# Operand buffers of a projection and an attention as tiles of their own, with unused words between them

## The chip, the core and the metric

The kernel runs on one core of one Trainium2 chip. The time is the device time of one launch in microseconds. Two runs of the kernel before took 3833.39 and 3838.01 us, median 3835.7. Times below are counted from the start of the profiled execution's span.

## The reference

The reference is a two-layer trunk over 2304 tokens (256 of context, 2048 latent) of width 1024, in float32. Per layer:

```python
h = layer_norm(x) * (1.0 + scale) + shift
(hq, hff, hfb, hi, hgate, mcq, mckv, mkr, mgate,
 gq, gk, gv, gaf, gab, ggate) = split_cols(h @ w_in)
hg_lat, hg_ctx = bidirectional_recurrence(...)     # HGRN2, chunks of 64
gla_lat, gla_ctx = bidirectional_recurrence(...)   # gated linear attention
mla_lat = blockwise_attend(q, k, v)                # softmax attention, latent q and kv
x_new = layer_norm(DEEPNORM_ALPHA * x + gate * (y @ w_out)) * ln_g + ln_b
```

`y` is the three groups' outputs, normed or gated, side by side. The context tokens get the same treatment in the first layer only. All products are float32; the kernel makes each from three one-pass products of a high and a low part: `a b = ah bh + ah bl + al bh`.

## The kernel before, in words

Each layer runs three stages: `project` (normed activations times the input weights, the results staged in DRAM), `mix` (attention and the two recurrences side by side) and `output` (output projection, residual, post norm). In time: layer 0's projection from about 48 to 698.5 us, its mix to about 1640, its output to 1992; layer 1's projection from 1993 to 2611, its mix to about 3500, its output to the end.

**Projection.** Nine pairs of token tiles (256 tokens) in three blocks; for each block, twelve weight groups of 224 or 256 columns run against the block's pairs. `split_pair` (L396) turns a pair's activations `hf` into `hh` and `hl` ([128, 8, 256] each, four of either), `group_weights` (L342) loads a weight group and turns it into `wh` and `wl` (two of either). `group` (L404) has two forms of product: `natural` (L411, matmul L417) holds the tokens of h stationary and streams 256 weight columns; `transposed` (L421, matmul L428) holds 128 weight columns stationary and streams the 256 tokens. An L417 or L428 matmul is named `pj` after its result. ScalarE makes the high parts (a cast, through the helper `split`, L73 to L83, so many casts have line L77) and VectorE the low parts (L83), and ScalarE or VectorE stage the results (`stg`) for DRAM.

**Mix.** `mix` (L945) first reads the keys and values back from DRAM, in five pieces of 512 tokens (the last of 256) each: `cth`, `ctl`, `ks` for the scores, `cnh`, `cnl` for the weighted sum. Each piece passes through a raw buffer `kraw`; `kraw` and the query's `cq` share two buffers. `query_group` (L819) prepares two token tiles' queries: `cq` is split, multiplied into `pq` (24 matmuls, L838) and `pr` (12), 8 transposes give `ptq`, and the results are `qh`, `ql`, `rh`, `rl`. `attend` (L869) makes the scores `pss` from five products (L888 to L892: `cth qh`, `ctl qh`, `cth ql`, `ks rh`, `ks rl`), the exponentials `sx`, their transposes `ptp`, split into `ph` and `pl`, and the weighted sum `oc` (L913 to L917). The recurrences (`back_states`, `recur`) run between.

**Memory.** `Route` (L40) makes one pool per string that it is given, one behind the other in memory; a tag's buffers come from the pool that names the tag. A pool's space is given back at the end of a stage, and a tile placed there later waits for the users of exactly the tiles that it overlaps. In `project` of before, `hh hl` come first and `wh wl` last, above everything that mix or output uses. Byte offsets in a partition: hh at 33,376 + 8192 i, hl at 66,144 + 8192 i; wh at 196,384 and 204,576, wl at 212,768 and 220,960 in layer 0 (544 lower in layer 1); mix's cth, ctl, ks at 112,224 to 139,872; output's lnb, z, xto and wob between 91,008 and 136,064.

**Order of the work.** A scheduler places each instruction on its engine by priority and by when its inputs and buffers are expected to be ready; engines run in that order. `AHEAD` = 600 (L953) lets mix's key loads and first query come earlier than the place where they are written, `EARLY` = 1000 (L290) does so for the first weights and activations of layer 1's projection.

Of the kernel before, what the change touches and what calls it, by code (L numbers as in the profile page):

```python
# [7 lines left out]
F32 = mybir.dt.float32  # L8
F32R = mybir.dt.float32r
# [7 lines left out]
P = 128  # L17
# [14 lines left out]
def view(ap, offset, dims, parts=None):  # L32
    """A free-dimension pattern of its own on the tile behind ap."""
    pd = list(ap.ap[0])
    if parts is not None:
        pd[1] = parts
    return bass.AP(ap.tensor, ap.offset + offset, [pd] + [list(d) for d in dims])


class Route:  # L40
    """Tiles by tag, each from the pool that holds the tag: the order of pools is the order in memory."""
# [12 lines left out]
class Trunk:  # L54
# [17 lines left out]

    def split(self, hi, lo, src, hi_eng="act", lo_eng="dve"):  # L73
        """src = hi + lo with both parts in the tensor engine's one-pass format."""
# [10 lines left out]
    def rsqrt(self, pool, v, n, name):  # L85
        """(v + eps already added) ** -0.5 for a [P, n] tile."""
        r = pool.tile([P, n], F32, tag=name, name=name)
        self.nc.gpsimd.tensor_tensor(r, v, self.mhalf[:, :n], op=ALU.pow)
        return r

    def constants(self):
# [5 lines left out]
        # the gated heads' query scale, on the rows of the even and of the odd heads  # L97
# [11 lines left out]
    def scratch(self, l):  # L109
        """Layer l's arrays in DRAM, and its modulation columns."""  # L110
# [25 lines left out]
    def mod_first(self, S, R, ps, first):  # L136
        """Layer 0's shift and scale as columns."""
        nc, io = self.nc, self.io
        pm = [ps.tile([2, 512], F32, tag="pj", bufs=4, name="pm") for _ in range(4)]
        for k in range(KD):  # L140
            w = R.tile([P, 2 * D], F32, tag=("hh", "hl")[k % 2], bufs=4, name="wmod")
# [19 lines left out]
    def mod_rest(self, S0, S1, R, bm0):  # L161
        """Layer 0's gate and layer 1's modulation: products along the free dimension, one column block at a time."""
# [30 lines left out]
        bm = R.tile([P, 24], F32, name="bmd")  # L193
# [10 lines left out]
    def lower_bounds(self, S):  # L204
        """Layer 1's forget-gate floor: the running sum of the softmax over layers less its first term."""
# [20 lines left out]
    def gate_weights(self, l, S, R):  # L226
        """The low-rank gate weights stacked [hi; hi; lo], against gates stacked [hi; lo; hi]."""
# [9 lines left out]
    def latent_weights(self, l, S, R, ps):  # L237
        """The low-rank query and key weights joined: M_h = W_uq,h W_uk,h^T; and the rotary and value ones."""
# [28 lines left out]
    def project(self, l, S, after):  # L267
        """after: the next layer's arrays, where its modulation is worked out beside this projection."""
        nc, io = self.nc, self.io
        with ExitStack() as ctx:  # L270
            R = Route(lambda: self.pool(ctx), "hh hl", "stg gcat gq gkv",
                      "zaT ltn lkd zn zh ltt lqn jk ss rsk rsq ropt ropa ropb gxs gab",
                      "srow wmt jkm mp mc bmc bmd gcol pad", "wraw", "xt st mv ve rs hf", "wh wl")
            ps = Route(lambda: self.pool(ctx, psum=True), "tz", "pj", "tr", "px")
            npair = self.ntiles // 2
            blocks = [list(range(p0, min(p0 + 3, npair))) for p0 in range(0, npair, 3)]
            # the first two weight groups run side by side while the first block's tokens come in
# [9 lines left out]
            else:  # L287
                pad = R.tile([P, 64 * 64], F32, name="pad")
# [48 lines left out]
    # weight groups in the order in which they run: first column, number of columns  # L337
# [4 lines left out]
    def group_weights(self, l, R, g, first=False):  # L342
# [3 lines left out]
        wh = R.tile([P, KD, 256], F32R, tag="wh", bufs=2, name="wh")  # L346
        wl = R.tile([P, KD, 256], F32R, tag="wl", bufs=2, name="wl")
# [7 lines left out]
    def normed_pair(self, l, S, R, ps, pr, plain=False):  # L355
        """The modulated norm of two token tiles, transposed: [d, k, 256]; plain leaves out the modulation."""
# [39 lines left out]
    def split_pair(self, R, hf, hi_eng="dve"):  # L396
        hh = R.tile([P, KD, 256], F32R, tag="hh", bufs=4, name="hh")
        hl = R.tile([P, KD, 256], F32R, tag="hl", bufs=4, name="hl")
# [5 lines left out]
    def group(self, l, S, R, ps, g, w, h, pairs):  # L404
        """One weight group against a block's token pairs; yields after each pair."""
# [4 lines left out]
        def natural(pr):  # L410
            """[P, tile of the pair, 256]: tokens on partitions, n weight columns."""  # L411
# [9 lines left out]
        def transposed(pr):  # L421
            """[P, 128-column block, 256]: weight columns on partitions, the pair's tokens."""
# [12 lines left out]
        def by_tile(o):  # L435
            """[P, block, tile, 128] on a stage that holds tile by tile."""
# [58 lines left out]
    def rope(self, pool, out, src, t, per_tile):  # L495
        """Rotary positions by rows and columns. src [P, n, 64]; out [P, n, 2, 64] holds the result twice.
        n counts tiles from t on (per_tile), or heads of tile t."""
# [23 lines left out]
    def rms(self, pool, pj, n, tag):  # L521
        """[P, 2] reciprocal RMS over n columns of each tile of the pair."""
# [8 lines left out]
    def key_latents(self, S, pp, ps, pj, pr, xs):  # L531
        """RMS norm and rotary positions of a pair's key latents, and their transposes; the forget gates' inputs."""
# [52 lines left out]
    def gla_decay(self, S, pp, xs, pairs):  # L585
        """The forget gates exp(log_sigmoid(x) / 16), both directions of a block."""
# [14 lines left out]
    def head_rows(self, h):  # L601
        """(key slice in a [.., 3*128] natural tile, output rows, output column block, value block)"""
# [6 lines left out]
    def chunk_products(self, rp, rps, kT, vt, name):  # L609
        """Chunk by chunk [P, block, 64]: sum over the chunk's tokens of key x value for all heads."""  # L610
# [583 lines left out]
```

## Time and profile before

| | |
|---|---|
| runs, median | 3835.7 us |
| profiled execution, own span | 3840.8 us |
| TensorE (PE) busy | 3740.7 us, 97% |
| VectorE (DVE) busy | 2529.3 us, 66% |
| ScalarE (ACT) busy | 1452.2 us, 38% |
| GpSimd (POOL) busy | 187.3 us, 5% |
| mean granted TensorE clock | 0.989 |

A matmul's busy time in the profile (about 0.28 us for 256 columns) is longer than the distance between two starts, because matmuls overlap in the array; the distance between starts is read from the order in time. A clock of 1.00 is 2.4 GHz, 0.50 is 1.2 GHz.

### The profile page before, as it was taken

How to read it: one execution, taken by the hardware profiler on the slowest of the kernel's cores; microseconds unless marked ns; L12 is line 12 of the kernel's file. 1: busy time of each engine (PE TensorE's matmuls, PEld its weight loads, DVE VectorE, ACT ScalarE, POOL GpSimd, SP SyncE). 2: the span in 40 equal slices, each digit the busy share in tenths (PEclk: the TensorE clock that was granted, in tenths of full speed). 3: DMA queues.
4: the chain of work that ended last, by engine and by line, in shares of the span. 5: the costliest groups of instructions: out<-in, count | busy, mean ns of one | idle time of the engine just before them, and what ended most of it. 6: DMA issues, size and time to landing. Idle time of an engine off the chain costs nothing.

```text
span 3840.8 us, 82784 instructions
## 1 busy us (share of the span) xinstructions
PE 3740.7 (97%) x34152; PEld 3341.4 (87%) x34152; DVE 2529.3 (66%) x6956; ACT 1452.2 (38%) x2347; POOL 187.3 (5%) x194
## 2 busy tenths in 40 slices
PE   8899999999999999998999999999999999999899
PEld 5899999888888888887879999998888888888777
DVE  6763242577888888776765432426778888888566
ACT  3524242344444444442115252523444444444400
POOL 1000000000000000010110000000000000000111
PEclk9999999999999999999999999999999999999999
DMA  7775453323222212114435453523231212211232
GB/s 253 229 206 155 122 155 108 110 85 92 76 68 62 69 57 69 54 59 167 150 105 181 141 156 101 170 90 118 78 96 49 79 55 69 73 55 33 89 140 104
DMA packets 305850, 415.30 MB, mean 108 GB/s; under 512 B 43008, under 2 KB 235840, under 8 KB 304448
## 3 DMA queue, kind: packets, MB, share of 16 engines
q1 hardware_dynamic: 304032, 407.64, 33.8%
q8 instruction: 269, 4.41, 0.5%
q10 hardware_dynamic: 1440, 2.36, 0.2%
q14 instruction: 109, 0.89, 0.1%
HBM read 290.89 MB, written 119.03 MB: 107 GB/s over the span
## 4 chain that ended last, share of the span: by engine, by line
PE 71%; DVE 2%; DMA 2%; ACT 1%; issue 0%; POOL 0%; SPq 0%; DVEq 0%; ACTq 0%; POOLq 0%
PE pj L417 10%; PE pa L774 7%; PE ptp L924 6%; PE pj L428 5%; PE oc L917 4%; PE oc L913 4%; PE pzo L1069 3%; PE pzo L1070 3%; PE pzo L1071 3%; PE pss L888 3%; PE oc L914 3%; PE pss L889 3%; PE pss L891 3%; PE pss L890 3%; PE pss L892 3%; PE po L801 1%
## 5 line engine op out<-in xcount | busy, mean ns | idle before, releaser
L417 PE MATMUL pj<-wh,hl 128*128 128x256 f32 (+1 forms) x2224 | 623.0, 281 | 8.4 <-DVE hl L83 8.4
L417 PE MATMUL pj<-wh,hh 128*128 128x256 f32 (+1 forms) x2224 | 624.5, 281 | 2.0 <-DVE ve L369 1.2
L417 PE MATMUL pj<-wl,hh 128*128 128x256 f32 (+1 forms) x2224 | 623.1, 280 | 0.0
L77 ACT CAST ph<-ptp 128x512 fp32r<-128x512 f32 x580 | 333.2, 586 | 369.9 <-PE ptp L924 349.6
L83 DVE TENSOR_TENSOR pl<-ptp,ph 128x512 fp32r<-128x512 f32 x580 | 392.9, 686 | 111.2 <-ACT ph L77 109.9
L893 DVE TENSOR_SCALAR_CACHE_REDUCE sx<-pss 128x512 f32<-128x512 f32 (+1 forms) x648 | 399.2, 631 | 79.5 <-PE pss L892 74.2
L417 PEld LDWEIGHTS pj<-wh,hl 128*128 128x128 f32 x2224 | 421.5, 190 | 9.3 <-DVE hl L83 9.3
L417 PEld LDWEIGHTS pj<-wh,hh 128*128 128x128 f32 x2224 | 423.1, 190 | 2.7 <-DVE ve L369 1.6
L417 PEld LDWEIGHTS pj<-wl,hh 128*128 128x128 f32 x2224 | 422.3, 190 | 0.0
L924 PE MATMUL ptp<-ident,sx 128*128 128x128 f32 x2320 | 368.5, 275 | 17.2 <-ACT sx L903 17.2
L903 ACT ACTIVATE sx<-sx,nm 128x2304 f32<-128x2304 f32 (+1 forms) x136 | 288.4, 2121 | 173.5 <-DVE nm L899 171.4
L913 PE MATMUL oc<-ph,cnh 128*128 128x256 f32 x1160 | 346.0, 320 | 5.1 <-ACT ph L77 4.4
L83 DVE TENSOR_TENSOR wl<-wraw,wh 128x1024 fp32r<-128x1024 f32 (+1 forms) x144 | 169.6, 1211 | 238.8 <-ACT wh L77 238.7
L428 PE MATMUL pj<-hh,wh 128*128 128x256 f32 x1136 | 321.0, 283 | 0.0
L428 PE MATMUL pj<-hh,wl 128*128 128x256 f32 x1136 | 319.3, 281 | 0.0
L428 PE MATMUL pj<-hl,wh 128*128 128x256 f32 x1136 | 318.2, 280 | 0.0
L914 PE MATMUL oc<-ph,cnl 128*128 128x256 f32 x1160 | 301.9, 282 | 0.0
L924 PEld LDWEIGHTS ptp<-ident,sx 128*128 128x128 f32 x2320 | 272.8, 141 | 28.0 <-ACT sx L903 19.4
L774 PE MATMUL pa<-qa,km 64*64 64x64 f32 (+1 forms) x4896 | 279.3, 248 | 3.4 <-DVE qa L739 3.1
L888 PE MATMUL pss<-cth,qh 128*128 128x512 f32 (+1 forms) x648 | 269.4, 416 | 5.4 <-DVE sx L893 5.0
L917 PE MATMUL oc<-pl,cnh 128*128 128x256 f32 x1160 | 251.1, 297 | 7.0 <-DVE pl L83 6.8
L774 PEld LDWEIGHTS pa<-qa,km 64*64 64x64 f32 x4896 | 202.4, 134 | 58.4 <-issue 34.3
(241 smaller groups left out, 8035.7 us busy)
## 6 DMA issues: line engine op xcount, KB each, us to landing
wraw<-in_w_in_dram SPq DMA_DIRECT2D x132, 512.0 KB, 4.7
dnat<-stg SPq DMA_DIRECT2D x104, 256.0 KB, 2.1
vg<-dnat SPq DMA_DIRECT2D x34, 512.0 KB, 4.2
yt<-dy SPq DMA_DIRECT2D x34, 512.0 KB, 3.6
wmt<-in_w_modT_dram SPq DMA_DIRECT2D x64, 256.0 KB, 4.0
fa<-dF SPq DMA_DIRECT2D x36, 384.0 KB, 3.3
ka<-dK SPq DMA_DIRECT2D x36, 384.0 KB, 3.3
dK<-stg SPq DMA_DIRECT2D x36, 256.0 KB, 4.1
```

Of the source, the lines that this page charges most:

```text
L77: nc.scalar.copy(hi, src)
L83: nc.vector.tensor_tensor(lo, src, hi, op=ALU.subtract)
L417: nc.tensor.matmul(pj[:, j, :n], h[pr][a][:, k, tk], w[b][:, k, :n], start=(k == 0 and a + b == 0), stop=(k == KD - 1 and a == 1))
L428: nc.tensor.matmul(pj[:, j, :], w[b][:, k, cs], h[pr][a][:, k, :], start=(k == 0 and a + b == 0), stop=(k == KD - 1 and b == 1))
L774: nc.tensor.matmul(pa[rows, po:po + n], km[rows, sl, tk:tk + 64], mv, start=True, stop=True, tile_position=(64 * e, 64 * e))
L888: nc.tensor.matmul(pss[:, :n], G["qh"][hp][:, i, tk], K["cth"][:, ks], start=True, stop=False)
L893: nc.vector.tensor_scalar(sx[:, ks], pss[:, :n], SCALE, None, op0=ALU.mult, op1=ALU.max, accum_out=mx[:, nb:nb + 1])
L903: nc.scalar.activation(sx[:, :nk], sx[:, :nk], AF.Exp, bias=nm, accum_out=sm)
L913: nc.tensor.matmul(oc, K["cnh"][:, ks], ph[:, c, :], start=(kc + c == 0), stop=False)
L914: nc.tensor.matmul(oc, K["cnl"][:, ks], ph[:, c, :], start=False, stop=False)
L917: nc.tensor.matmul(oc, K["cnh"][:, ks], pl[:, c, :], start=False, stop=(kc + c == nch - 1))
L924: nc.tensor.transpose(pt[:, c, i, :], pexp[i][:, (kc + c) * P:(kc + c + 1) * P], self.ident)
```

## The change

In `project`, `wh` and `wl` move from the last pool to right behind `hh` and `hl`, and every one of the four `hh`, four `hl`, two `wh`, two `wl` becomes a tag with a pool of its own, in the order hh0 hl0, hh1 hl1, hh2 hl2, hh3 hl3, wh0 wl0, wh1 wl1. Four more tiles, of 8 to 64 words, stand between these pairs (all but hh3 and wh0); `fill` writes one column of each and nothing reads them. In `mix`, the same is done to qh and ql (four) and ph and pl (two), with gaps of 16 to 48 words; in layer 1 another one stands ahead of `rh rl`.

The new byte offsets in layer 0's projection: hh at 33,376, 49,824, 66,272 and 82,720, each hl 8192 behind; wh0 at 99,104, wl0 at 107,296, wh1 at 115,520, wl1 at 123,712 to 131,904. In layer 1: wh0 at 99,008, wl0 at 107,200, wh1 at 115,648, wl1 at 123,840 to 132,032. Mix's cth, ctl and ks lie at 112,416 to 140,064 (layer 0; 128 lower in layer 1).

The instructions are the same on all engines but GpSimd, which gets 17 memsets. Comments and docstrings are dropped, so line numbers shift (L77 becomes L83 in the changed kernel, L83 becomes L89, L966 becomes L984).

```diff
+    def fill(self, pool, *names):
+        for name in names:
+            n = int(name.split("_")[1])
+            self.nc.gpsimd.memset(pool.tile([P, n], F32, name=name)[:, 0:1], 0.0)
...
-            w = R.tile([P, 2 * D], F32, tag=("hh", "hl")[k % 2], bufs=4, name="wmod")
+            w = R.tile([P, 2 * D], F32, tag=f"h{'hl'[k % 2]}{k // 2 % 4}", name="wmod")
...
-        bm = R.tile([P, 24], F32, name="bmd")
+        bm = R.tile([P, 24], F32, tag="bmc", name="bmd")
...
-            R = Route(lambda: self.pool(ctx), "hh hl", "stg gcat gq gkv",
+            self.nh, self.nw = 0, 0
+            gaps = ("ha_16", "hb_16", "hc_16", "wa_8") if l == 0 else ("ha_8", "hb_8", "hc_8", "wa_64")
+            R = Route(lambda: self.pool(ctx), "hh0", "hl0", gaps[0], "hh1", "hl1", gaps[1], "hh2", "hl2", gaps[2],
+                      "hh3", "hl3", "wh0", "wl0", gaps[3], "wh1", "wl1", "stg gcat gq gkv",
                       "zaT ltn lkd zn zh ltt lqn jk ss rsk rsq ropt ropa ropb gxs gab",
-                      "srow wmt jkm mp mc bmc bmd gcol pad", "wraw", "xt st mv ve rs hf", "wh wl")
+                      "srow wmt jkm mp mc bmc bmd gcol pad", "wraw", "xt st mv ve rs hf")
+            self.fill(R, *gaps)
...
-                pad = R.tile([P, 64 * 64], F32, name="pad")
+                pad = R.tile([P, 62 * 64], F32, name="pad")
...
-        wh = R.tile([P, KD, 256], F32R, tag="wh", bufs=2, name="wh")
-        wl = R.tile([P, KD, 256], F32R, tag="wl", bufs=2, name="wl")
+        wh = R.tile([P, KD, 256], F32R, tag=f"wh{self.nw % 2}", name="wh")
+        wl = R.tile([P, KD, 256], F32R, tag=f"wl{self.nw % 2}", name="wl")
+        self.nw += 1
...
-        hh = R.tile([P, KD, 256], F32R, tag="hh", bufs=4, name="hh")
-        hl = R.tile([P, KD, 256], F32R, tag="hl", bufs=4, name="hl")
+        hh = R.tile([P, KD, 256], F32R, tag=f"hh{self.nh % 4}", name="hh")
+        hl = R.tile([P, KD, 256], F32R, tag=f"hl{self.nh % 4}", name="hl")
+        self.nh += 1
...
-            ap = Route(lambda: self.pool(ctx), "os mx nm sm ri", "mg", "ym", "ph pl", "cth ctl ks", "cq cqh cql",
-                       "qn ropt ropa ropb", "rh rl", "qh ql", "cnh cnl", "sx")
+            self.nq, self.np = 0, 0
+            gaps = ("pa_48", "qa_16", "qb_16", "qc_16", "") if l == 0 else ("pa_16", "qa_16", "qb_16", "qc_16", "ra_32")
+            ap = Route(lambda: self.pool(ctx), "os mx nm sm ri", "mg", "ym", "ph0", "pl0", gaps[0], "ph1", "pl1", "cth ctl ks", "cq cqh cql",
+                       "qn ropt ropa ropb", gaps[4], "rh rl", "qh0", "ql0", gaps[1], "qh1", "ql1", gaps[2], "qh2",
+                       "ql2", gaps[3], "qh3", "ql3", "cnh cnl", "sx")
+            self.fill(ap, *[g for g in gaps if g])
```

The tags qh, ql, ph and pl change in `query_group` and `attend` as hh and hl do in `split_pair`.

The scheduler's order moves with the buffers. First place: ScalarE at the end of layer 0's projection. Of the kernel before, where the first casts of the keys stand among the projection's stages (`stg`) and weight casts:

```order
L453 ACT_TABLE_LOAD
L453 ACTIVATE stg<-pj 128x2x2x128
L77 CAST cth<-kraw 128x512 x2
L77 CAST wh<-wraw 128x1024 x2
L453 ACTIVATE stg<-pj 128x2x2x128
L77 CAST cth<-kraw 128x512 x2
L459 ACT_TABLE_LOAD
L459 ACTIVATE stg<-pj 128x2x2x128
L460 ACTIVATE stg<-pj 128x2x2x128
L77 CAST cth<-kraw 128x256
L77 CAST cqh<-cq 128x512
```

Of the changed kernel, the same casts (line L83 there; `DMA kraw` are loads that ScalarE's queue issues):

```order
L497 ACTIVATE stg<-pj 128x512 x3
L83 CAST wh<-wraw 128x1024 x2
L497 ACTIVATE stg<-pj 128x512 x6
L83 CAST cth<-kraw 128x512 x4
L83 CAST cth<-kraw 128x256
L984 DMA kraw<-dkT_92 128x512
L83 CAST cqh<-cq 128x512
L984 DMA kraw<-dkT_92 128x512
L986 CAST ks<-kraw 128x512
L984 DMA kraw<-dkT_92 128x512
L986 CAST ks<-kraw 128x512
L83 CAST qh<-pq 128x512
```

The casts of cth, which stood ahead of the projection's last weight groups, now stand behind its last six stages; behind these rows come the other ks, qh, three cnh, then the first rh. TensorE in the changed kernel, at the same place, behind the last pj and the first query products:

```order
L903 MATMUL pss<-cth,ql 128x512 x2
L863 MATMUL pr<-urh_1183,cqh 128x256
L863 MATMUL pr<-url_1184,cqh 128x256
L863 MATMUL pr<-urh_1183,cql 128x256
L863 MATMUL pr<-urh_1183,cqh 128x256
L863 MATMUL pr<-url_1184,cqh 128x256
L863 MATMUL pr<-urh_1183,cql 128x256
L874 MATMUL ptq<-ident,qn 128x128 x4
L904 MATMUL pss<-ks,rh 128x512 x2
L863 MATMUL pr<-urh_1183,cqh 128x256
L863 MATMUL pr<-url_1184,cqh 128x256
L863 MATMUL pr<-urh_1183,cql 128x256
```

In the kernel before, pq, pr and ptq stand between matmuls of the projection, and the first pss directly behind its last pj.

Second place: VectorE between layer 0's output and layer 1's projection. Of the kernel before, from the last half tile of output on:

```order
L1072 TENSOR_TENSOR z<-pzo,gate 128x512
L1073 SCALAR_TENSOR_TENSOR z<-xto,z 128x512
L1075 BN_STATS sto<-z 128x6
L1077 BN_AGGR mvo<-sto 128x2
L1079 TENSOR_SCALAR veo<-mvo 128x1
L1086 SCALAR_TENSOR_TENSOR z<-z,mvo,lng 128x1024
L232 CAST wa_24131<-wa2r 96x256
L1089 SCALAR_TENSOR_TENSOR z<-z,rso,lnb 128x1024
L233 TENSOR_TENSOR wa_24131<-wa2r,wa_24131 32x256
L83 TENSOR_TENSOR hl<-hf,hh 128x1024 x4
```

Of the changed kernel, the same half tile (L1090 is the first step of z there, L1107 the last), in two pieces that follow on each other:

```order
L1090 TENSOR_TENSOR z<-pzo,gate 128x512
L89 TENSOR_TENSOR hl<-hf,hh 128x1024
L238 CAST wa_24313<-wa2r 96x256
L89 TENSOR_TENSOR wl<-wraw,wh 128x1024
L1091 SCALAR_TENSOR_TENSOR z<-xto,z 128x512
L85 CAST hh<-hf 128x1024
L239 TENSOR_TENSOR wa_24313<-wa2r,wa_24313 32x256
L85 CAST hh<-hf 128x1024
L1093 BN_STATS sto<-z 128x6
L89 TENSOR_TENSOR hl<-hf,hh 128x1024
```

```order
L376 BN_STATS st<-xt 128x6 x2
L89 TENSOR_TENSOR hl<-hf,hh 128x1024
L1095 BN_AGGR mvo<-sto 128x2
L376 BN_STATS st<-xt 128x6 x2
L378 BN_AGGR mv<-st 128x2
L89 TENSOR_TENSOR wl<-wraw,wh 128x1024
L1097 TENSOR_SCALAR veo<-mvo 128x1
L1104 SCALAR_TENSOR_TENSOR z<-z,mvo,lng 128x1024
L378 BN_AGGR mv<-st 128x2
L380 TENSOR_SCALAR ve<-mv 128x1
L1107 SCALAR_TENSOR_TENSOR z<-z,rso,lnb 128x1024
```

Between the steps of the last z there now stand splits of the activations and weights and statistics for layer 1. On ScalarE the casts of the first weight group (`wh` 128x4x224) of layer 1, which stood ahead of most of the output stage's casts, now stand behind all of the output stage:

```order
L83 CAST yhl<-pty 128x512
L83 CAST hh<-hf 128x1024 x2
L83 CAST wh<-wraw 128x1024
L397 ACTIVATE hf<-pt,shT_97,scT_96 128x256 x8
L83 CAST wh<-wraw 128x1024
L83 CAST wh<-wraw 128x4x224 x2
L539 ACTIVATE jk,ss<-pj 128x128 x2
```

The first pj of layer 1 in TensorE's changed order is one of those with the 224-column group.

## Rows read from the trace of the kernel before

**Rows 1.** The page: span, engines (busy us, share, instructions), the chain that ended last.

```profile
span 3840.8 us, 82784 instructions
...
PE 3740.7 (97%) x34152; PEld 3341.4 (87%) x34152; DVE 2529.3 (66%) x6956; ACT 1452.2 (38%) x2347; POOL 187.3 (5%) x194
...
PE pj L417 10%; PE pa L774 7%; PE ptp L924 6%; PE pj L428 5%; PE oc L917 4%; PE oc L913 4%; PE pzo L1069 3%; PE pzo L1070 3%; PE pzo L1071 3%; PE pss L888 3%; PE oc L914 3%; PE pss L889 3%; PE pss L891 3%; PE pss L890 3%; PE pss L892 3%; PE
```

**Rows 2.** Windows by layer: us, PE, PEld (x), clock, DMA; L417, then L428.

```profile
48.00:698.50 650.50, 410.80 (x3456) 402.83 (x3456) 0.99 0.53 158
1993.00:2610.80 617.80, 391.98 (x3216) 384.58 (x3216) 0.99 0.43 136
...
48.00:698.50 650.50, 207.13 (x1728) 204.59 (x1728) 0.99 0.53 158
1993.00:2610.80 617.80, 205.38 (x1680) 202.75 (x1680) 0.99 0.43 136
```

**Rows 3.** Timeline of PE: start us, us, engine, line; first and last of runs.

```profile
599.77 0.28 PE L417 MATMUL pj<-wh,hh 128*128 128x256 f32 x1
...
600.91 0.28 PE L417 MATMUL pj<-wl,hh 128*128 128x256 f32 x1
...
2149.80 0.28 PE L417 MATMUL pj<-wl,hh 128*128 128x256 f32 x1
...
2150.99 0.28 PE L417 MATMUL pj<-wh,hl 128*128 128x256 f32 x1
...
529.73 0.28 PE L428 MATMUL pj<-hl,wh 128*128 128x256 f32 x1
...
530.90 0.28 PE L428 MATMUL pj<-hh,wl 128*128 128x256 f32 x1
...
2079.74 0.28 PE L428 MATMUL pj<-hh,wh 128*128 128x256 f32 x1
...
2080.94 0.28 PE L428 MATMUL pj<-hl,wh 128*128 128x256 f32 x1
...
698.50 0.39 PE L888 MATMUL pss<-cth,qh 128*128 128x512 f32 x1
...
700.59 0.39 PE L892 MATMUL pss<-ks,rl 128*128 128x512 f32 x1
```

**Rows 4.** Timeline of ACT: first and last casts of ks, layer 0.

```profile
556.04 0.62 ACT L968 CAST ks<-kraw 128x512 fp32r<-128x512 f32 x1 [2.32 <-DMA kraw<-dkT]
...
565.25 0.94 ACT L968 CAST ks<-kraw 128x512 fp32r<-128x512 f32 x2
```

**Rows 5.** Loads of kraw from 600 to 740 us, issue to landing.

```profile
DMA to landing us min/median/max: 3.6/4.6/4.7
```

**Rows 6.** Windows at mix's start: us, PE, PEld, DVE, ACT, POOL, clock, DMA, GB/s.

```profile
700.00:730.00 30.00, 24.81 (x185) 18.30 (x184) 23.56 (x75) 10.36 (x14) 0.49 (x5) 0.89 0.82 251
2610.00:2640.00 30.00, 26.11 (x202) 19.20 (x201) 25.29 (x80) 10.86 (x15) 1.08 (x9) 0.94 0.79 252
```

**Rows 7.** Timeline of PE at layer 1's start; in brackets the idle before.

```profile
1999.70 0.55 PE L417 MATMUL pj<-wh,hl 128*128 128x224 f32 x1 [6.20 <-DVE hl L83]
```

**Rows 8.** Timeline of DVE at layer 1's start.

```profile
1992.44 0.69 DVE L1072 TENSOR_TENSOR z<-pzo,gate 128x512 f32<-128x512 f32 x1 [3.44 <-PE pzo L1071]
...
1996.65 1.28 DVE L1089 SCALAR_TENSOR_TENSOR z<-z,rso,lnb 128x1024 f32<-128x1024 f32 x1 [0.17 <-POOL rso L88]
...
1998.42 4.63 DVE L83 TENSOR_TENSOR hl<-hf,hh 128x1024 fp32r<-128x1024 f32 x4
```

**Rows 9.** Stores of z from 1960 to 2012 us, issue to landing.

```profile
L1091 SPq DMA_DIRECT2D xs<-z x4: 319/319/333, 1963.7 to 1998.0; - x4
...
DMA to landing us min/median/max: 2.6/2.6/3.0
```

**Rows 10.** Timeline of ACT: casts of layer 1's first weights.

```profile
1773.20 2.73 ACT L77 CAST wh<-wraw 128x896 fp32r<-128x896 f32 x3
```

**Rows 11.** Window behind the idle of layer 1's start: us, PE, clock, DMA, GB/s.

```profile
2000.00:2010.00 10.00, 10.00 (x69) 0.74 0.44 126
```

**Rows 12.** Groups by line and shape: count, busy us, mean ns, idle before.

```profile
L888 PE MATMUL pss<-cth,qh 128*128 128x512 f32 x512 | 222.3, 434 | 3.9 <-DVE sx L893 3.5
```

More of the change, by code (lines that the diff above doesn't have):

```diff
@@ L829, in query_group @@
         for hp in range(2):
-            qh = ap.tile([P, 2, 256], F32R, tag="qh", bufs=4, name="qh")
-            ql = ap.tile([P, 2, 256], F32R, tag="ql", bufs=4, name="ql")
+            qh = ap.tile([P, 2, 256], F32R, tag=f"qh{self.nq % 4}", name="qh")
+            ql = ap.tile([P, 2, 256], F32R, tag=f"ql{self.nq % 4}", name="ql")
+            self.nq += 1
             pq = aps.tile([P, 2, 256], F32, tag="mi", name="pq")
@@ L924, in attend @@
                         nc.tensor.transpose(pt[:, c, i, :], pexp[i][:, (kc + c) * P:(kc + c + 1) * P], self.ident)
-                ph = ap.tile([P, 2, 256], F32R, tag="ph", bufs=2, name="ph")
-                pl = ap.tile([P, 2, 256], F32R, tag="pl", bufs=2, name="pl")
+                ph = ap.tile([P, 2, 256], F32R, tag=f"ph{self.np % 2}", name="ph")
+                pl = ap.tile([P, 2, 256], F32R, tag=f"pl{self.np % 2}", name="pl")
+                self.np += 1
                 self.split(ph, pl, pt.rearrange("p c i n -> p c (i n)"))
```

## The prediction

> **What bounds the kernel now.** I read the page's busy shares first, then the chain of waits. The tensor engine is busy in 97% of the span, and the chain that ends last runs through it for 71%, the projection's two matmul lines ahead [rows 1]. So a saving must come out of matmul time, and idle time added to that engine lengthens the program one for one. The change touches both: it moves the operands of nearly every large matmul, and it moves buffers on top of others, so that waits appear. Since a busy matmul engine is not one at its peak, I read next how far apart matmuls start in steady stretches, then the two places where one stage hands over to the next.
>
> The projection's matmuls (128 stationary columns, 256 moving columns) number 3456 and 1728 in layer 0, 3216 and 1680 in layer 1 [rows 2]. Ten starts apart, L417 takes 599.77 to 600.91 in layer 0, 114 ns each, and 2149.80 to 2150.99 in layer 1, 119 ns. L428 takes 117 ns (529.73 to 530.90) and 120 ns (2079.74 to 2080.94). The attention's 512-column products take 2.09 us for nine, 232 ns [rows 3]. At the granted 2.4 GHz, 256 columns would be 106.7 ns and 512 would be 213.3. So some ns per matmul are open, and the same form differs between layers, whose buffers lie at different addresses.
>
> **The change, part by part.** *The gaps.* Each rotating copy gets its own offset. No row shows the new offsets, so I bound them. If every projection matmul went to the best spacing seen, 114 ns: 1728 x 3 + 3216 x 5 + 1680 x 6 ns = 31 us gained. If all went to the worst, 120: 3456 x 6 + 1728 x 3 + 3216 x 1 = 29 us lost. The new offsets are mixed: some hh copies repeat an offset of before and most do not, so layer 0's L417 can lose its 114 while layer 1 can gain it. I take **0**, midway between two nearly equal ends. The Trainium skill (SBUF — State Buffer, section "SBUF: two separate sides") says that TensorE never waits on anyone at the SBUF and that weight loads have a second, independent read port. By that rule the term is exactly 0 and the range loses both ends. The 114 against 119 ns of one form does not settle it, but speaks against reading the rule as "all spacings are equal".
>
> *The new place of wh and wl, at the end of a projection.* They lay above everything; now they end at byte 131,904 of a partition in layer 0, and mix's cth, ctl and ks (112,416 to 140,064) lie over wl0, wh1 and wl1. These three could be made while the projection still ran. In the order of before, the first cth cast stands among layer 0's stages, long ahead of the end; in the changed order all five stand behind the last six stages of the projection, the query work (24 pq, 12 pr, 8 transposes) behind its last matmul, and the products with rh behind that. The trace shows what this work costs where it is hidden: five ks chunks from 556.04 to 566.2, 2.0 us each, through two load buffers [rows 4]; the last kraw loads land 4.6 us after their issue, at the busy start of mix [rows 5].
>
> The new chain: after the last projection matmul a stage cast, its store and six recurrence loads are issued ahead of kraw, about 3.4 us; first landing 4.6 later, at 8. Then 13 more tiles through the same two buffers up to the cast of rh (5 cth, one cq, 5 ks, 3 cnh in all): 26 us at 2.0 each. rh at 34; at 2.6 us a tile, which a busier queue would give, at 42. I take **35**. Taken off:
> - The query work now lies in this hole, no longer in the projection: 44 instructions at 0.118 = 5.2 us.
> - Six score products run before rh: 6 x 0.232 = 1.4.
> - The idle that stands there already: 30 - 24.8 = 5.2 us in layer 0 and 30 - 26.1 = 3.9 in layer 1 [rows 6].
>
> That is 35 - 5.2 - 1.4 - 5.2 = **23 us in layer 0**, and 35 - 5.2 - 1.4 - 3.9 = **24 us in layer 1**. Lower end: two loads in flight, limited only by casts and landings at 0.9 us a tile, 8 + 12 = 20 instead of 35, so 8 and 10. Upper end: 42, so 30 and 32.
>
> *The start of layer 1's projection.* Here wh0 and wl0 (99,008 to 115,392) lie over the output stage's lnb, z and xto, and wh1 and wl1 over wob. Before, the weights were cast well ahead; the one wait was 6.20 us for hl, to 1999.70 [rows 7], 7.3 us after the first step of the last z chain. Now the first pj needs the cast of wh0, which needs the last z written to memory. On the vector engine the last z chain, 5.5 us (1992.44 to 1997.94), stood alone [rows 8]. In the changed order, three hl and two wl (1.16 us each), two hh and four statistics (0.69 each, as a z step of that size) and about 0.8 us of small ones stand between its steps: 5.8 + 4.1 + 0.8 = 10.7. So z ends 16.2 us after the first step. Its store takes 0.3 to issue and 2.6 to 3.0 to land [rows 9], 19.4; the cast of wh0 takes 0.9 [rows 10], and three handovers between engines about 0.5 together (an estimate): **20.8** instead of 7.3, **+13.5 us**. It could be +8 if half of those instructions find their inputs late and so leave the z chain alone, and +18 if the store lands late behind weight loads and the slower clock lasts: its stretch after the present hole shows 0.74 [rows 11].
>
> *The rest.* 17 memsets of one column on GpSimd, which is busy in 5% of the span: 0, hidden beside all else, and on the path only if a matmul waited for one, which the order shows nowhere. ph, pl, qh, ql with tags of their own rotate over as many buffers as before: 0. The smaller pad and bmd's shared tag: 0.
>
> **Sum**, against the profiled execution's own 3840.8: 0 + 23 + 24 + 13.5 = +60.5, 3901.3. The median of the runs stands 5.1 below that execution, so **3896 us**, 1.6% slower. What a measurement here can tell from no change is about 2%, below 3759 or above 3912.
>
> **The rivals.**
> 1. *The gaps pay more than the holes cost* (the other side: not slower, and perhaps faster). Mechanism: the offset of the stationary against the moving operand sets the spacing. For: one form at 114 and 119 ns. Against: both offsets lie in rows of before without any at 107. At 106.7 ns the projection would gain 3456 x 7.3 + 1728 x 10.3 + 3216 x 12.3 + 1680 x 13.3 = 105 us; the scores (5 lines of x512 each [rows 12]) 2560 x 18.7 = 48 us. With the holes that is 3896 - 153 = 3743 at the outer end, and 3820 at half of it. It decides from 60 us, about 5 ns on each of 12,600 matmuls. Chance 0.22, of which 0.06 is faster than 3759. The Trainium skill (TensorE: Matmul & The Clock Gate, section "Wait — 56ns, not 53.3ns?") gives N / 2.4 GHz + 2.5 ns between starts, 109.2 and 215.8 ns here; if the gaps restored that, by estimate it is some 120 us gained, 3776. The trace of before disagrees with the rule by 5 to 16 ns.
> 2. *Short holes.* The loads run at the lower end, other work fills the rest: 8 + 10 + 8 = 26, 3862, and 3836 if nothing of it is on the path. For: mix's start moves 251 GB/s in either layer [rows 6], so the queue can be quick once its loads are issued. Against: the tensor engine takes its work in order, and recurrence products stand behind the scores. Chance 0.12.
> 3. *Longer holes.* 42 us per layer, 18 at layer 1, and spacings at the worst end: 3835.7 + 30 + 32 + 18 and up to 29, 3916 to 3945. For: each hole sends the clock down and the first microseconds after it run at half speed. Chance 0.14.
>
> **How the numbers follow.** My forecast, 3896, has 0.52; its own range is 3865 to 3915. The range of 8 in 10 leaves out rival 1's outer half and rival 3's upper half: 3818 to 3920. Faster by over 2%: 0.06. Slower by over 2%: rival 3's 0.14 and 0.06 of the forecast, 0.20. Within 2%: 0.74.
>
> **What will show it.** In the changed profile: idle time of the tensor engine of 20 to 35 us behind the last pj of each layer, released by the cast of rh or by kraw loads, with kraw issued only then; 12 to 20 us idle ahead of layer 1's first pj, released by the cast of wh; the counts of matmuls unchanged, their starts at 114 to 120 ns. If these starts fall to 110 or less, rival 1 holds and the forecast is wrong by its price; if kraw is issued well before the last pj, the reading of the overlay is wrong.

## The result, and the profile after

| | before | changed |
|---|---|---|
| median of the runs | 3835.7 us | 3927.36 us (3926.81, 3927.91) |
| profiled execution, own span | 3840.8 us | 3926.1 us |

The ratio is 1.0241, 95% interval 1.0212 to 1.0271: slower by 92 us, where I had forecast 60 and a range up to 3920. The spans alone differ by 85 us; the profiled execution of before stood 5 us above its runs' median, that of the changed kernel 1 below.

The page of the changed kernel, as in [rows 1]:

```profile
span 3926.1 us, 82846 instructions
...
PE 3758.6 (96%) x34152; PEld 3349.4 (85%) x34152; DVE 2532.0 (64%) x6956; ACT 1453.5 (37%) x2347; POOL 185.0 (5%) x211
...
PE 69%; DVE 4%; DMA 2%; ACT 1%; issue 0%; SPq 0%; POOL 0%; DVEq 0%; ACTq 0%; POOLq 0%
```

The matmuls' busy time rose by 18 us only; the engine's share fell. So most of the loss is idle time. The list of waits of TensorE (waiter, releaser: us in total, times, longest) names it:

```profile
PE pq L851 <- ACT cqh L83: 42.2, 2, 21.1
PE pzo L1087 <- DVE z L1090: 17.1, 2, 10.7
PE pj L429 <- ACT wh L83: 17.1, 1, 17.1
```

Neither the first nor the third stood in the list of before; the second came to 9.8 us there. TensorE in order of time, behind the last pj of layer 0, at layer 1's start, and behind the last pj of layer 1:

```profile
699.04 0.27 PE L429 MATMUL pj<-wh,hl 128*128 128x256 f32 x1
720.41 0.58 PE L851 MATMUL pq<-cqh,mh 128*128 128x256 f32 x1 [21.09 <-ACT cqh L83]
...
737.48 1.22 PE L904 MATMUL pss<-ks,rh 128*128 128x512 f32 x2 [1.64 <-ACT rh L83]
...
2054.92 1.01 PE L429 MATMUL pj<-wh,hh 128*128 128x224 f32 x3 [17.07 <-ACT wh L83]
...
2677.00 0.58 PE L851 MATMUL pq<-cqh,mh 128*128 128x256 f32 x1 [21.08 <-ACT cqh L83]
...
2695.51 1.22 PE L904 MATMUL pss<-ks,rh 128*128 128x512 f32 x2 [0.67 <-ACT rh L83]
```

In layer 0 the products with rh start 38.4 us behind the last pj. The loads and casts ahead of them (SyncE's queue, then ScalarE):

```profile
703.32 0.80 SPq L984 DMA_DIRECT2D kraw<-dkT  x2
...
707.61 1.24 ACT L83 CAST cth<-kraw 128x512 fp32r<-128x512 f32 x2 [7.61 <-DMA kraw<-dkT]
...
736.85 0.58 ACT L83 CAST rh<-ptq 128x512 fp32r<-128x512 f32 x1
```

kraw is issued only behind the last pj, 4.3 us after it, and 14 tiles pass through the two buffers before rh: 33.5 us from the issue to the cast of rh. The first 60 us behind the last pj, of before and then of the changed kernel (the columns of [rows 6]):

```profile
698.40:758.40 60.00, 54.78 (x435) 44.53 (x433) 43.78 (x135) 24.60 (x35) 1.17 (x10) 0.94 0.48 145
2610.70:2670.70 60.00, 55.79 (x455) 45.33 (x454) 46.37 (x141) 25.61 (x36) 1.27 (x11) 0.97 0.48 152
```

```profile
699.10:759.10 60.00, 30.07 (x189) 23.40 (x188) 32.99 (x86) 20.11 (x31) 0.88 (x7) 0.72 0.50 147
2655.70:2715.70 60.00, 29.22 (x153) 22.96 (x153) 31.16 (x82) 19.39 (x30) 0.88 (x7) 0.69 0.49 144
```

25 and 27 us more idle time, and the granted clock falls from 0.94 and 0.97 to 0.72 and 0.69. The moved query work (5.2 us) sits inside. Much of the low clock lies in the idle time itself, where it costs nothing. The 30 us from the first product with rh on, in the changed kernel:

```profile
737.48:767.48 30.00, 28.49 (x236) 23.17 (x237) 24.81 (x80) 12.61 (x18) 0.29 (x3) 0.87 0.39 115
2695.51:2725.51 30.00, 28.84 (x234) 23.38 (x235) 24.23 (x77) 12.77 (x18) 0.29 (x3) 0.85 0.37 113
```

There 0.87 and 0.85 stand against the 0.89 and 0.94 of [rows 6], and 1.5 and 1.2 us of idle time against 5.2 and 3.9.

At the handover to layer 1, VectorE and ScalarE, which answer to [rows 7 to 9]:

```profile
2036.15 0.68 DVE L1090 TENSOR_TENSOR z<-pzo,gate 128x512 f32<-128x512 f32 x1
...
2049.88 1.28 DVE L1107 SCALAR_TENSOR_TENSOR z<-z,rso,lnb 128x1024 f32<-128x1024 f32 x1 [0.31 <-POOL rso L94]
```

```profile
2053.93 1.78 ACT L83 CAST wh<-wraw 128x896 fp32r<-128x896 f32 x2 [7.96 <-DMA xs<-z]
```

The last z chain is stretched over 15.0 us instead of 5.5, the cast of wh waits for the store of z, the first pj for that cast.

Spacing, as in [rows 3]: L429 (the L417 of before) in layer 0, and L440 (L428) in layer 1, ten starts apart:

```profile
399.43 0.28 PE L429 MATMUL pj<-wh,hh 128*128 128x256 f32 x1
...
400.61 0.28 PE L429 MATMUL pj<-wl,hh 128*128 128x256 f32 x1
...
2119.74 0.28 PE L440 MATMUL pj<-hh,wh 128*128 128x256 f32 x1
...
2120.91 0.28 PE L440 MATMUL pj<-hl,wh 128*128 128x256 f32 x1
```

118 and 117 ns: the first was 114, the second 120. The mean over all neighbouring pairs of 256 columns that start less than 140 ns apart: L417 in layer 0 from 114.4 to 118.2, in layer 1 118.2 and 118.1; L428 in layer 0 117.6 and 118.0, in layer 1 from 120.0 to 117.8.

### The profile page after: what moved, and what is told of

The parts are those of the page before. It is cut to its first block, busy times and chain, and to the rows that moved or that the text cites. A ratio compares the mean times of both kernels' runs of the same rounds, so it can differ in the third digit from the quotient of the medians.

```text
span 3926.1 us, 82846 instructions
## 1 busy us (share of the span) xinstructions
PE 3758.6 (96%) x34152; PEld 3349.4 (85%) x34152; DVE 2532.0 (64%) x6956; ACT 1453.5 (37%) x2347; POOL 185.0 (5%) x211
## 4 chain that ended last, share of the span: by engine, by line
PE 69%; DVE 4%; DMA 2%; ACT 1%; issue 0%; SPq 0%; POOL 0%; DVEq 0%; ACTq 0%; POOLq 0%
PE pj L429 10%; PE pa L786 7%; PE ptp L937 5%; PE pj L440 5%; PE oc L930 4%; PE oc L926 3%; PE pzo L1087 3%; PE pzo L1088 3%; PE pzo L1089 3%; PE pss L901 3%; PE oc L927 3%; PE pss L904 3%; PE pss L902 3%; PE pss L903 3%; PE pss L905 3%; PE po L813 1%
## 5 line engine op out<-in xcount | busy, mean ns | idle before, releaser
L429 PE MATMUL pj<-wh,hh 128*128 128x256 f32 (+1 forms) x2224 | 626.8, 282 | 17.1 <-ACT wh L83 17.1
L429 PE MATMUL pj<-wh,hl 128*128 128x256 f32 (+1 forms) x2224 | 625.2, 281 | 0.7 <-DVE hl L89 0.7
L429 PE MATMUL pj<-wl,hh 128*128 128x256 f32 (+1 forms) x2224 | 625.2, 281 | 0.0
L83 ACT CAST ph<-ptp 128x512 fp32r<-128x512 f32 x580 | 332.5, 586 | 376.4 <-PE ptp L937 361.9
L89 DVE TENSOR_TENSOR pl<-ptp,ph 128x512 fp32r<-128x512 f32 x580 | 392.7, 687 | 113.3 <-ACT ph L83 111.9
L429 PEld LDWEIGHTS pj<-wh,hh 128*128 128x128 f32 x2224 | 422.2, 190 | 17.3 <-ACT wh L83 17.3
L429 PEld LDWEIGHTS pj<-wh,hl 128*128 128x128 f32 x2224 | 421.8, 190 | 1.0 <-DVE hl L89 1.0
L429 PEld LDWEIGHTS pj<-wl,hh 128*128 128x128 f32 x2224 | 422.2, 190 | 0.0
L89 DVE TENSOR_TENSOR wl<-wraw,wh 128x1024 fp32r<-128x1024 f32 (+1 forms) x144 | 169.4, 1210 | 248.0 <-ACT wh L83 247.9
L440 PE MATMUL pj<-hh,wh 128*128 128x256 f32 x1136 | 321.3, 283 | 0.0
L440 PE MATMUL pj<-hh,wl 128*128 128x256 f32 x1136 | 320.0, 282 | 0.0
L440 PE MATMUL pj<-hl,wh 128*128 128x256 f32 x1136 | 319.6, 281 | 0.0
```

The costliest lines, as they stand in the source:

```text
L83: nc.scalar.copy(hi, src)
L89: nc.vector.tensor_tensor(lo, src, hi, op=ALU.subtract)
L429: nc.tensor.matmul(pj[:, j, :n], h[pr][a][:, k, tk], w[b][:, k, :n], start=(k == 0 and a + b == 0), stop=(k == KD - 1 and a == 1))
L440: nc.tensor.matmul(pj[:, j, :], w[b][:, k, cs], h[pr][a][:, k, :], start=(k == 0 and a + b == 0), stop=(k == KD - 1 and b == 1))
```

## The experiments

The first five take the change apart; the others ask what the gaps do. The kernel before was run beside each: 3836.4 us beside the first seven and the first scan, 3836.2 beside the second scan and the difference of 64, 3838.5 beside the last.

**Gaps without the move.** wh and wl back on top of memory, all else as changed:

```diff
-                      "hh3", "hl3", "wh0", "wl0", gaps[3], "wh1", "wl1", "stg gcat gq gkv",
+                      "hh3", "hl3", "stg gcat gq gkv",
...
-                      "srow ...", "wraw", "xt st mv ve rs hf")
+                      "srow ...", "wraw", "xt st mv ve rs hf", "wh0", "wl0", gaps[3], "wh1", "wl1")
```

> The changed kernel with wh and wl (still tiles of their own with their gap) back in the last pool, where they lie over nothing that mix or output needs early. All other gaps stay. Theory 'holes' (the loss is waiting at the three handovers, because buffers came to lie on each other): the two holes behind the projections and the one ahead of layer 1's are gone, first pss directly behind the last pj; what is left is the spacing of the projection's matmuls at their new offsets, some +8 us: 3835 to 3850. Rival 'offsets' (the gaps themselves slow the matmuls, the holes only replace idle time that was there): stays at 3900 or more.

3840.17 us, ratio 1.0011 (1.0002 to 1.0020). All three holes are gone, the first pss stands directly behind the last pj in both layers, and the gaps cost 4 us: theory "holes".

```profile
702.09 0.28 PE L430 MATMUL pj<-wh,hl 128*128 128x256 f32 x1
702.21 0.40 PE L902 MATMUL pss<-cth,qh 128*128 128x512 f32 x1
...
2605.58 0.28 PE L430 MATMUL pj<-wh,hl 128*128 128x256 f32 x1
2605.70 0.39 PE L902 MATMUL pss<-cth,qh 128*128 128x512 f32 x1
```

**The move without the gaps.** The kernel before with

```diff
-            R = Route(lambda: self.pool(ctx), "hh hl", "stg gcat gq gkv",
+            R = Route(lambda: self.pool(ctx), "hh hl", "gap", "wh wl", "stg gcat gq gkv",
...
-                      "srow ...", "wraw", "xt st mv ve rs hf", "wh wl")
+                      "srow ...", "wraw", "xt st mv ve rs hf")
+            nc.gpsimd.memset(R.tile([P, 48 if l == 0 else 40], F32, name="gap")[:, 0:1], 0.0)
...
-                pad = R.tile([P, 64 * 64], F32, name="pad")
+                pad = R.tile([P, 62 * 64], F32, name="pad")
```

> The kernel before with wh and wl moved right behind hh and hl and with one gap that keeps the offsets of wh and wl against hh and hl (modulo 256 bytes) as they were in each layer; no gap between the rotating buffers. Theory 'holes': all of the loss, 3900 to 3925, holes of 26 us behind each projection and about 21 us ahead of layer 1's first pj. Rival 'offsets': as before, 3830 to 3845.

3916.28 us, ratio 1.0215 (1.0200 to 1.0230). The first and third entry of the changed kernel's list of waits are there again:

```profile
PE pq L839 <- ACT cqh L77: 43.8, 2, 22.4
...
PE pj L418 <- ACT wh L77: 10.7, 2, 9.7
```

The move alone makes 80 of the 91 us. One part of the expectation missed: the hole ahead of layer 1's first pj came to 11.0 us from the last output matmul (9.7 in the list), not about 21.

**Keys and their loads elsewhere.** The changed kernel with mix's memory in another order:

```diff
-            ap = Route(..., "ph1", "pl1", "cth ctl ks", "cq cqh cql", ..., "ql2", gaps[3], "qh3", "ql3", "cnh cnl", "sx")
+            ap = Route(..., "ph1", "pl1", "sx", "cnh cnl", "cq cqh cql", ..., "ql2", gaps[3], "qh3", "ql3", "cth ctl ks")
```

> The changed kernel with mix's pools in another order (sx and the value operands cnh, cnl where cth, ctl, ks were; the raw buffers kraw and cq behind them; cth, ctl, ks at the end), so that neither the keys nor their raw buffers lie over the weights or over the projection's stages. Theory 'holes': the holes behind both projections go, the one of 21 us ahead of layer 1 stays: 3927 less 55 to 70 = 3857 to 3872. Rival 'offsets': no difference from the changed kernel, 3920 to 3930.

3856.74 us, ratio 1.0059 (1.0042 to 1.0076), 70.6 less than the changed kernel. The wait of pq has left the list, the first cast of cth is back beside the projection, and the wait at layer 1's start is untouched:

```profile
PE pj L429 <- ACT wh L83: 17.0, 1, 17.0
...
544.78 0.81 SPq L984 DMA_DIRECT2D kraw<-dkT  x2
...
547.58 0.62 ACT L83 CAST cth<-kraw 128x512 fp32r<-128x512 f32 x1 [4.02 <-DMA kraw<-dkT]
```

**Keys alone elsewhere**, the raw buffers where the change put them:

```diff
-            ap = Route(..., "ph1", "pl1", "cth ctl ks", "cq cqh cql", ..., "cnh cnl", "sx")
+            ap = Route(..., "ph1", "pl1", "sx", "cq cqh cql", ..., "cnh cnl", "cth ctl ks")
```

> The changed kernel with sx and the keys cth, ctl, ks exchanged in mix's memory: the keys no longer lie over the weights, but their raw buffers kraw and cq stay where they are, over the projection's stage buffers stg. Theory 'keys over weights' (what the prediction named): the holes behind the projections go, 3857 to 3872. Rival 'raw buffers over stages' (the loads, not the keys, are what waits): the holes stay, 3915 to 3930, with kraw issued only behind the last stage.

3924.64 us, ratio 1.0234 (1.0219 to 1.0249): nothing is won. The loads still wait for the projection's end:

```profile
PE pq L851 <- ACT cqh L83: 41.8, 2, 21.0
...
L984 SPq DMA_DIRECT2D kraw<-dkT x5: 319/431/537, 702.0 to 713.8; - x5
```

What the prediction named, keys over weights, is not needed for the loss. The stages moved too: the pool of `stg`, which the projection uses to its end, now begins where wl1 ends (131,904 in layer 0). The four stg buffers lie at 135,488 to 143,680 there, and the raw buffers, at 140,064 to 144,160, lie over the last two.

**Loads alone elsewhere**, the keys over the weights:

```diff
-            ap = Route(..., "ph1", "pl1", "cth ctl ks", "cq cqh cql", ..., "cnh cnl", "sx")
+            ap = Route(..., "ph1", "pl1", "cth ctl ks", "sx", "cq cqh cql", ..., "cnh cnl")
```

> The changed kernel with only the raw buffers kraw and cq (and what follows them) moved up behind sx, off the projection's stages; the keys cth, ctl, ks stay over wl0, wh1 and wl1. Theory 'either overlay is enough': the loads can be issued early, but the casts into cth still wait for the last pj; the holes shrink by the first issue and landing, some 8 of 28 us each, 3905 to 3920. Rival 'only the raw buffers matter': 3857 to 3872 as with both moved.

3896.85 us, ratio 1.0158 (1.0144 to 1.0171), below the 3905 that I expected at least. The first two loads go out early, the casts into cth do not:

```profile
PE pq L851 <- ACT cqh L83: 33.2, 2, 16.9
...
545.57 0.91 SPq L984 DMA_DIRECT2D kraw<-dkT  x2
...
L83 ACT CAST cth<-kraw x5: 404/617/619, 701.7 to 715.8; 128x512 fp32r<-128x512 f32 x4, 128x256 fp32r<-128x256 f32 x1
```

So either overlay is enough for a hole: as differences of runs, the raw buffers over the stages cost 3924.6 - 3856.7 = 68 us alone, the keys over the weights 3896.9 - 3856.7 = 40, both together 71. These are not prices of the holes alone. With the loads out early the first product with rh still comes 34.0 and 36.4 us behind the last pj, only 4.4 and 3.5 earlier than in the changed kernel. The new order of mix's memory shifts other waits too: at the start of the output stages, TensorE waits 14.5 us for `yt` in the kernel with both moved and 20.5 with the keys alone moved, but 1.6 here and 1.9 in the changed kernel. So the shorter hole is 8 of the 30.5 us won over the changed kernel; the rest is not explained.

**What the gaps set.** In the traces of before and of the changed kernel I sorted the distances between starts of the projection's matmuls by the address of a matmul's moving operand less that of the next one's stationary operand (which is loaded meanwhile), modulo 256 bytes. The mean distance in ns:

| difference | 0 | 32 | 64 | 96 | 128 | 160 | 192 | 224 |
|---|---|---|---|---|---|---|---|---|
| ns | 119.7 | 116.9 | 117.2 | 120.0 | 118.6 | 118.1 | 114.8 | 118.4 |

Before, L417 is at 192 in layer 0 and 160 in layer 1, L428 at 64 and 96. In the changed kernel and in the one with the gaps alone, a difference of 0 occurs with both operands at 32, 160 or 192 modulo 256 and reads 119.6 to 119.8 ns in each, and one of 96 occurs with the moving operand at five places and reads 119.8 to 119.9: it is the difference that counts, not the place of one operand. A matmul's own stationary operand lies at the same place modulo 256 as the next one's in all but about 100 of 9,000 pairs, so these kernels do not tell the next one's from its own. The next kernels change these differences in the kernel before and, but for a memset or a smaller `pad` that makes room, nothing else.

*Layer 1's weights 32 bytes up*:

```diff
-                      "srow ...", "wraw", "xt st mv ve rs hf", "wh wl")
+                      "srow ...", "wraw", "xt st mv ve rs hf", "gap", "wh wl")
+            if l > 0:
+                nc.gpsimd.memset(R.tile([P, 8], F32, name="gap")[:, 0:1], 0.0)
```

> The kernel before with 8 unused words ahead of wh and wl in layer 1 only: moving operand less next stationary operand becomes 192 (L417) and 64 (L428) modulo 256 bytes, as in layer 0, instead of 160 and 96. Theory 'the difference of the two operands' addresses modulo 256 bytes sets the spacing': L417 in layer 1 from 118.2 to about 114.5 ns, L428 from 120 to 117.7: 3216 x 3.7 + 1680 x 2.3 = 16 us less, 3821. Rival 'the two reads of the tensor engine are independent, layers differ for another reason': 3836 as before.

3823.33 us, ratio 0.9963 (0.9949 to 0.9976). L417 in layer 1 goes to 114 ns (mean 114.6), L428 to a mean of 117.1:

```profile
2149.43 0.28 PE L419 MATMUL pj<-wl,hh 128*128 128x256 f32 x1
...
2150.57 0.28 PE L419 MATMUL pj<-wh,hl 128*128 128x256 f32 x1
```

*Difference 0 everywhere* (the same edit, 16 words in layer 0, 24 in layer 1):

> The kernel before with 16 unused words ahead of wh and wl in layer 0 and 24 in layer 1: the difference is 0 modulo 256 bytes in both layers and both forms. Theory 'difference modulo 256 bytes': every projection matmul at about 119.7 ns: 3456 x 5.3 + 1728 x 2.1 + 3216 x 1.5 - 1680 x 0.3 = 26 us more, 3862. Rival 'independent reads': 3836.

3859.39 us, ratio 1.0063 (1.0049 to 1.0076). All four means are 119.9 ns:

```profile
2149.51 0.28 PE L418 MATMUL pj<-wl,hh 128*128 128x256 f32 x1
...
2150.71 0.28 PE L418 MATMUL pj<-wh,hl 128*128 128x256 f32 x1
```

Both signs come out as the difference says, within 3 us of the sums.

*Two scans*, in which the weights begin a step further on in a larger tile from group to group of layer 1:

```diff
+        o = 4 * (self.nw % 16) if l > 0 else 0          # second scan: 32 + self.nw % 16
-        wh = R.tile([P, KD, 256], F32R, tag="wh", bufs=2, name="wh")
+        wh = R.tile([P, KD * 256 + 64], F32R, tag="wh", bufs=2, name="wh")
+        wh = wh[:, o:o + KD * 256].rearrange("p (k n) -> p k n", k=KD)
...
```

The same is done to wl; `self.nw` counts the weight groups, and the larger tiles are there in layer 1 only.

> The kernel before, where in layer 1 each weight group's wh and wl begin 0, 16, 32, ... or 240 bytes into a larger tile, one step on from group to group: one look at the spacing at sixteen differences. Theory 'difference modulo 256 bytes': spacings from 114 to 120 ns by difference, best at 192 or close to it, the steps between (odd multiples of 16) between their neighbours; mean near 118, time 3830 to 3842. Rival 'independent reads': one spacing throughout.

3834.52 us, one run. Means by difference and form from 113.3 to 120 ns (123 in one group); L417 at difference 64 and L428 at 192 read 113.3 and 113.4.

> The kernel before, where in layer 1 each weight group's wh and wl begin 128, 132, ... or 188 bytes into a larger tile: differences from 32 to 92 (L417) in steps of 4 bytes. Theory 'fine steps matter': single differences under 112 ns, down to 107 or so. Rival 'only coarse steps matter, 113 is the floor': 113 to 120 ns, the best at 64 again.

3838.17 us, one run. Between 113.8 and 122 ns, none near 107. Neither side of the expectation had it: steps of 4 bytes do change the spacing, and the best was not at 64, where L417 now read 117.8, but 113.8 at 204 for L428.

*Difference 64 for L417, 192 for L428* (the same edit as for 0, 32 words in layer 0, 40 in layer 1):

> The kernel before with 32 unused words ahead of wh and wl in layer 0 and 40 in layer 1: wh less hh is 64 modulo 256 bytes, so that moving less next stationary is 64 for L417 and 192 for L428, the two pairs that the scan showed at 113.3 ns. Theory 'difference modulo 256 bytes': all projection matmuls near 113.4: 3456 x 1.0 + 1728 x 4.3 + 3216 x 4.8 + 1680 x 6.6 = 37 us less than before, 3799, and faster than the kernel before and the changed one. Rival 'the scan's best pairs do not hold for a whole stage (113.3 was a lucky phase of short runs)': 3815 to 3836.

3826.03 us, ratio 0.9975 (0.9966 to 0.9984). That is the rival's range. L428 goes to 114.8 and 114.3, near the 113.4 expected, but L417 to 116.8 and 117.0: most of it runs at 118 as below. The 113.3 of the scan did not hold for a stage, as the rival said.

```profile
2149.49 0.28 PE L418 MATMUL pj<-wl,hh 128*128 128x256 f32 x1
...
2150.67 0.28 PE L418 MATMUL pj<-wh,hl 128*128 128x256 f32 x1
```

*192 for both forms in layer 1*: o is 8 words for the groups of L417 and 40 for those of L428.

> The kernel before, where in layer 1 wh and wl lie in tiles 64 words larger and begin 8 words in for the weight groups of L417 and 40 words in for those of L428: moving less next stationary is 192 modulo 256 bytes for both forms in layer 1; layer 0 stays (192 for L417, 64 for L428). Theory 'the difference 192 holds for whole stages, 64 does not': L417 at about 114.5 ns, L428 at about 114.4: 3216 x 3.7 + 1680 x 5.6 = 21 us less than before, 3815. Rival 'the spacing at one difference changes from build to build': 3820 to 3836.

3821.62 us, ratio 0.9958 (0.9944 to 0.9971), the fastest kernel here, though not told apart from the shift by 32 bytes, and in the rival's range. L417 in layer 1 at 114.3; L428 at 116.2, not the 114.4 expected. Why L428 takes 114.3 at this difference in one build and 116.2 in another stays open.

## Why the prediction was wrong, point by point

Which places lose, and by waiting, was right; the size was not. With 3836.4 for the kernel before, the runs split the 91 us:

| term | predicted | measured, as a difference of runs |
|---|---|---|
| behind both projections | 23 + 24 = 47 | 3927.4 - 3856.7 = 70.7 |
| ahead of layer 1's projection | 13.5 | 3856.7 - 3840.2 = 16.5 |
| offsets and the rest | 0 | 3840.2 - 3836.4 = 3.8 |

1. **The step that failed is the hole behind the projections**, the terms 23 and 24, mis-sized by 24 us together. I ended the chain at the first products with rh, 35 us, took off idle time (5.2 and 3.9) and six score products (1.4), and assumed that from there all goes on as before. The traces show two parts of the miss.
   - *The chain* came out at 38.4 and 39.9 us, 8 us too many in both layers together: in layer 0, kraw was issued 4.3 us behind the last pj, not 3.4, and 33.5 us, not 30.6, passed from there to the cast of rh. (The long wait within it, 21.1 us, was ended by the cast of cqh; rh ended another 1.6.) The deductions nearly held. The first transposes of the exponentials come 52.9 and 54.7 us behind the last pj instead of 19.5 and 19.3, which, less the 5.2 us moved out of the projection, makes 28 and 30 us, 11 more than the terms, the chain's 8 among them.
   - *What comes later*, for which I had no term, is the other 13 us. Counted from the last pj to the last output matmul in layer 0 and to the program's end in layer 1, and less the same 5.2, the delay is 36 and 35 us, the 71 of the runs. Mix, from the first transposes to the last scores, ran 4.2 and 5.5 us longer, at a granted clock of 1.00 before and after (before first; its last scores come at 1743 and 3611 us, later than the ends of mix given at the start):

```profile
718.00:1743.00 1025.00, 1011.32 (x10855) 865.51 (x10855) 827.20 (x2645) 449.44 (x717) 38.10 (x34) 1.00 0.23 68
2630.00:3611.30 981.30, 968.28 (x10186) 830.09 (x10186) 784.90 (x2498) 427.97 (x668) 34.59 (x32) 1.00 0.22 67
...
752.00:1781.20 1029.20, 1013.46 (x10925) 862.08 (x10923) 831.35 (x2660) 449.66 (x718) 38.23 (x35) 1.00 0.23 68
2710.40:3697.20 986.80, 972.50 (x10257) 829.70 (x10255) 790.17 (x2513) 428.44 (x669) 34.68 (x33) 1.00 0.23 67
```

   In layer 0's output, the products wait 10.7 us for z where they waited 4.1. The kernel with the gaps alone, without any hole, loses 4 to 6 us against before over the same stretches, so this part need not come of the holes; its cause stays open. The slow clock, which stood in my text as a reason of the rival "longer holes", is not it: in the 30 us behind the first product with rh, 0.87 and 0.85 against 0.89 and 0.94 are 0.6 and 2.7 us, an estimate (30 us times the difference of the clocks).
2. **The cause of that hole was half seen.** I named the keys over the weights. Moving them alone won nothing; the raw buffers over the stages hold the loads back by themselves. I had read which tiles lie over wh and wl, not what had moved up behind them.
3. **The start of layer 1 was right** in place and mechanism: from the last output matmul to steady pj 21.2 us instead of 7.7 in the traces, +13.5 as in the sum; 16.5 between the runs. That the two agree so well is partly luck: from the first step of z, as the sum counts, it is 18.8 us and not 20.8, and that step came 2.5 us behind the last output matmul instead of 0.4. Interleaved work stretched z to 15.0 us (16.2 predicted); from there to the first pj took 3.8 us where the sum had 4.6, 0.5 of it for handovers, for which it named no row.
4. **The offsets, taken as 0**: by the means above and the counts, layer 0's L417 lost 3456 x 3.8 = 13 us and layer 1's L428 gained 1680 x 2.2 = 4. Both directions were in the prediction. In the run they come to 4 us with all else that the gaps move; the wait of 9.9 us for the DMA of uk in the list of before is not in that of the changed kernel.
5. **The median's 5.1 us** were rightly taken off: the result is compared with the runs' median, not with the one execution that was profiled. They are no part of the miss.
6. **Rival 1** had a true mechanism and a false price: the difference of two addresses does set the spacing, but over whole stages between 114 and 120 ns, never 107. By the Trainium skill (SBUF — State Buffer, section "SBUF: two separate sides") TensorE never waits on anyone there. The runs disagree: 119.9 ns throughout at difference 0 against 114.3 to 114.6 for L417 at 192 in the kernel before and its shifts. **Rival 3** gave 3916 to 3945 and so held the time, but by luck: its chain of 42 us came out at 38.4 and 39.9, its 18 us at layer 1 at 16.5 and its worst spacings at 118, and the slow clock that it gives as its reason cost about 3 us. The delay that comes later made up the difference. **Rival 2** is out: nothing filled the holes.

## What to carry to other kernels

Before a buffer is moved down in memory, list for every later tile under it which users it will now wait for, those of the pools that shift up behind it included, and ask of each whether it was loaded ahead of time. Price such a hole by the rate at which its loads come through their buffers (here 14 tiles in 33.5 us), and measure it to the end of the stage, not to the first instruction that runs: 13 of the 71 us came later. An offset between operands can be had by one small tile in front, without moving the buffers.

## What the runs showed of the hardware

The distance between float32 matmuls of 256 columns, each with its own stationary operand, followed the moving operand's address less that of the stationary operand (the next one's, or its own, which is not told apart), modulo 256 bytes: 119.9 ns at 0 in both forms and layers; for L417 at 192, 113.6 to 114.6 in the kernels without gaps between the copies and 115.6 to 116.1 in those with them. At 64, L417 read 113.3 in a short run and 117 over a stage, so the difference alone does not settle it. The 512-column products of attention showed no such range: 231 to 233 ns at differences 0, 64, 128 and 192.
